# A hybrid SSD and mixture-of-experts block: TensorE's order in the expert part written out by the program

## The chip, the cores and the metric

The kernel runs on one core of a Trainium2 chip. The metric is the device time of one execution in microseconds (us). A profile of one execution gives the busy time, the waits and the order of the instructions on five engines: PE (TensorE, with its weight loads shown as PEld), DVE (VectorE), ACT (ScalarE), POOL (GpSimd) and SP (SyncE, which here only starts transfers).

## What is computed

One decoder block on 512 tokens of width 1024: adaLN and a mixer (Mamba-2 SSD beside a gated short convolution), then adaLN and a mixture of experts. The change lies in the second part, of which the core is:

```python
def moe_ffn(h, router_w, router_bias, w_gate, w_up, w_down, sh_gate, sh_up, sh_down):
    ...
    _, e_idx = lax.top_k(jnp.where(expert_mask, biased, -jnp.inf), TOP_K)
    ...
    def expert_block(args):
        xb, e = args
        return (jax.nn.silu(xb @ w_gate[e]) * (xb @ w_up[e])) @ w_down[e]

    yb = lax.map(expert_block, (xin, block_expert)).reshape(n_rows, d)
    routed = jax.ops.segment_sum(yb * row_gate[:, None], row_tok, num_segments=T + 1)[:T]
    shared = (jax.nn.silu(hf @ sh_gate) * (hf @ sh_up)) @ sh_down
```

There are 64 experts of inner width 256, each token goes to 8 of them, and all is float32.

## The kernel before

The first 870 us hold the mixer, the routing and the shared expert. The rest is the expert part. The experts are ranked by their number of tokens and each gets a capacity by its rank (`CAPS`). Blocks of 128 token rows are formed from them: one expert with 128 rows, or two to four experts that share a block. A *unit* (`units`, made in the order of the string `ORDER`) is one to three such blocks with their experts; there are 32 units and 41 blocks. The letters are kinds of units: a (96 and 32 rows), p (2 x 64), q (4 x 32), f (one whole block), and y, z, x (one or two whole blocks and a shared one).

A unit's weights come in *pieces* of 512 KB per expert (`piece`, L842 and L845): four for gate and up (two of the eight chunks of the contraction each), two for down. SP loads them into a ring of 14 pages in a fixed order: pieces 1 to 3 of a unit, piece 0 of the next, then the unit's down pieces. A page comes free when its last reader is through.

For a whole block, ScalarE and VectorE split each weight page into a high and a low part (`split`, L130 and L132), and `matmul3` makes three whole-array matmuls of them (L125 to L127). For a shared block, `tiled` (L883 to L888) gives each expert a strip of 64 or 32 columns of the array, and the strips can run at the same time; the matmuls of these strips are at L887. Then, per block, `act_t` (L865) makes silu(gate) x up on ScalarE (L868) and VectorE (L869) and transposes it on TensorE through a PSUM bank of the pair `tr` (L122); ScalarE copies it out (L878, or L130 where it is split). The down product follows, and `done` scales it and splits it into a ring of three results.

`combine` (L1098 to L1114) adds results to the output with whole-array matmuls against one-hot token matrices (L1106, L1107), into the two PSUM banks `y`, which VectorE adds to `res` (L1112). It ran as soon as two results were there (`GRP`). `need_x` (L1266) and `xsplit` (L848) transpose the gathered tokens of a block, and `slots` (L1031) finds the tokens of a later block and starts its gather on POOL (L1055). `beyond` counts what exceeds the capacities, for a loop that does not run here.

`ffn` (L890) is a generator with a yield after each of the four gate/up pieces. The list `steps` takes the generators in turn: pieces 1, 2 and 3 of a unit, piece 0 of the next, the unit's down product. But this list is not TensorE's order: a scheduler takes the instructions of all engines and places each engine's by priority and by its own estimate of times. So transposes, combines and matmuls of different units are interleaved at fine grain.

Of the kernel before, what the change touches and what calls it, by code (L numbers as in the profile page):

```python
# [31 lines left out]
GRP = 2  # L32
XA = 3
# [4 lines left out]
AHEAD = 14  # L38
# [3 lines left out]
BEY = 100  # L42
# [11 lines left out]
PSPLIT = (3,)  # L54
NPS = 0
# [8 lines left out]
def block_kernel(ctx: ExitStack, tc: tile.TileContext, a, out, dbg=None):  # L64
# [657 lines left out]
    for j in range(KD):  # L722
# [7 lines left out]
        sg = wk()  # L730
# [134 lines left out]
    def act_t(o, whole):  # L865

        sg = rt.tile([P, FE], F32, name="sg", bufs=2)
        S.activation(sg, o[:, :FE], AF.Silu)  # L868
        V.tensor_tensor(sg, sg, o[:, FE:], op=OP.mult)  # L869
        tp = bank("tr", 2)  # L870
        av = sg.rearrange("p (f j) -> p j f", j=2)
        for j in range(2):
            transpose(tp[:, j * P:(j + 1) * P], av[:, j, :])
        aw = wkp.tile([P, 4, P], F32 if whole else FR, name="wkr", tag="wk")
        ah, al = aw[:, 0:2], aw[:, 2:4]
        tv = tp[:, :256].rearrange("p (j n) -> p j n", j=2)
        if whole:
            S.activation(ah, tv, AF.Copy)  # L878
        else:
            split_to(ah, al, tv)  # L880
        return ah, al
# [8 lines left out]
    def ffn(blocks, xs, w, done, gp=()):  # L890


        es = sorted({e for b in blocks for e in b})
        split_e = sorted({b[0] for b in blocks if len(b) == 1})
        os_ = [bank(*(("pj", 3) if i < 3 else ("y", 2))) for i in range(len(xs))]
        for q in range(4):
            us = {e: w(e, q) for e in es}
            hl_ = {e: split(us[e], GP if gp is True or q in gp else None) for e in split_e}
            for o, (xh, xl), b in zip(os_, xs, blocks):
# [6 lines left out]
            if q == 3:  # L906
                acts = [act_t(o, len(b) > 1) for o, b in zip(os_, blocks)]
            yield
        us = [{e: w(e, 4 + j) for e in es} for j in range(2)]
# [155 lines left out]
    def expert(blocks, sl_, xs, w, gp=()):  # L1065
# [3 lines left out]
        def done(b, n, o):  # L1069
# [18 lines left out]
            if n == 1:  # L1088
                parts.append(res_[b])
                if len(parts) == GRP and not tail[0]:  # L1090
                    combine()
# [3 lines left out]
    parts = []  # L1095
# [212 lines left out]
    need_x(1)  # L1308
    running, i1 = {}, 0
    for i, (u, j) in enumerate(steps):  # L1310
        if j == 0:
            i0 = ublk[id(u)]
            i1 = i0 + len(u[1])
            need_x(i1)
            running[id(u)] = expert([b for b, _ in u[1]], sl[i0:i1], xs[i0:i1],
                                    lambda e, q, n=unum[id(u)]: take((n, e, q), AHEAD),
                                    PSPLIT if unum[id(u)] < NPS else ())
        if i + XA < len(steps) and steps[i + XA][1] == 0 and len(xs) == i1:
            need_x(i1 + 1)
        if i == BEY:  # L1320
            ostart, oend, obase, nov = beyond()
        tail[0] = i == len(steps) - 1
        next(running[id(u)], None)
    combine(True)
# [101 lines left out]
```

## Time and profile before

| | before |
| --- | --- |
| median of 3 runs | 1614.7 us (1608.26 to 1615.08) |
| the profiled execution | 1601.06 us |
| its span, first to last instruction | 1599.3 us |
| PE busy in the span | 1525.1 us (95%) |
| DVE, ACT, POOL busy | 978.3, 643.3 and 312.5 us (61%, 40%, 20%) |
| bytes moved by DMA | 335.82 MB, mean 210 GB/s |

The share of an engine is taken over stages with different limits, so it has to be read stage by stage. Matmuls overlap in the array, so the sum of their durations is more than the time they cover; what counts is the distance of their starts.

### The profile page before, as it was taken

To read this page: it belongs to the slowest core of one execution; us is meant where nothing else is said; L and a number is where in the kernel's file an instruction comes from. 1 tells how busy PE (TensorE), PEld (TensorE's weight loads), DVE (VectorE), ACT (ScalarE), POOL (GpSimd) and SP (SyncE) were. 2 spreads that over 40 slices of the span, in tenths; PEclk is the share of its full clock that TensorE was granted. 3 is DMA by queue.
4 is the path that set the end of the run, shared out by engine and by line. 5 is a ranking of instruction groups with operands and counts; after the bars stand their busy time and mean duration, and the time that the engine had idled before them with its cause. 6 is when DMAs were issued, how large, how long until landed. Compare 5 with 4: busy or idle time off the path is not lost. (4 is left out here: it accounts for less than half of the span.)

```text
span 1599.3 us, 24806 instructions
## 1 busy us (share of the span) xinstructions
PE 1525.1 (95%) x8253; PEld 1009.2 (63%) x8253; DVE 978.3 (61%) x1760; ACT 643.3 (40%) x926; POOL 312.5 (20%) x314
## 2 busy tenths in 40 slices
PE   6999899999999999999988899999999999999996
PEld 4688787787787877888765445454454445446643
DVE  5557778667868656536786354564464456447646
ACT  3556575555634545434441323142233123223323
POOL 0011111011001456400035121221111212111211
PEclk9999999999999999999989999999999999999998
DMA  9763333534340677626363989787999799899991
GB/s 277 178 166 94 101 78 80 147 84 101 105 116 17 195 222 223 174 79 199 151 211 100 289 280 367 268 311 212 343 322 315 247 365 334 245 333 328 360 316 66
DMA packets 240599, 335.82 MB, mean 210 GB/s; under 512 B 18548, under 2 KB 141780, under 8 KB 240468
## 3 DMA queue, kind: packets, MB, share of 16 engines
q1 hardware_dynamic: 229380, 303.75, 59.3%
q0 software_dynamic: 11088, 30.45, 7.0%
q8 instruction: 67, 1.10, 0.3%
q14 instruction: 64, 0.52, 0.1%
HBM read 334.58 MB, written 4.28 MB: 212 GB/s over the span
## 5 line engine op out<-in xcount | busy, mean ns | idle before, releaser
L132 DVE TENSOR_TENSOR wl<-pg,wh 128x1024 fp32r<-128x1024 f32 (+1 forms) x201 | 245.5, 1226 | 164.2 <-ACT wh L130 163.8
L130 ACT ACTIVATE wh<-pg 128x1024 fp32r<-128x1024 f32 (+1 forms) x207 | 202.2, 987 | 232.5 <-PE ps_pj L126 101.9
L125 PE MATMUL ps_pj<-hm,wh 128*128 128x512 f32 x680 | 274.6, 405 | 2.1 <-ACT wh L130 2.1
L127 PE MATMUL ps_pj<-hm,wl 128*128 128x512 f32 x680 | 267.0, 393 | 5.5 <-DVE wl L132 5.5
L126 PE MATMUL ps_pj<-hm,wh 128*128 128x512 f32 x680 | 266.4, 392 | 0.0
L887 PE MATMUL ps_pj<-pg,xt 128*32 128x512 f32 (+1 forms) x1472 | 247.7, 600 | 0.0
L125 PEld LDWEIGHTS ps_pj<-hm,wh 128*128 128x128 f32 x680 | 128.1, 188 | 36.2 <-issue 5.5
L127 PEld LDWEIGHTS ps_pj<-hm,wl 128*128 128x128 f32 x680 | 128.0, 188 | 35.5 <-DVE wl L132 8.3
L126 PEld LDWEIGHTS ps_pj<-hm,wh 128*128 128x128 f32 x680 | 128.0, 188 | 28.8 <-issue 3.4
L887 PEld LDWEIGHTS ps_pj<-pg,xt 128*32 128x32 f32 (+1 forms) x1472 | 63.4, 115 | 110.8 <-issue 101.8
L1112 DVE TENSOR_TENSOR res<-res,ps_y 128x512 f32<-128x512 f32 x152 | 102.6, 686 | 42.1 <-PE ps_y L1107 40.4
L1083 DVE SCALAR_TENSOR_TENSOR wk<-ps_y,red,pg 128x512 f32<-128x512 f32 x82 | 61.1, 748 | 88.1 <-PE ps_y L887 57.1
L1055 POOL DMA_INDIRECT pg<-h_d,idx x41 | 49.8, 1215 | 326.7 <-DVE oh L1039 78.5
L887 PE MATMUL ps_y<-pg,wkr 128*32 128x512 f32 (+1 forms) x736 | 107.5, 596 | 2.0 <-DMA pg<-in_w_down_dram 2.0
L1079 POOL TENSOR_SCALAR oht<-iota_t,tok 128x512 fp32r<-128x512 f32 x41 | 67.1, 1642 | 129.1 <-PE ps_y L1107 128.9
L1107 PE MATMUL ps_y<-pg,oht 128*128 128x512 f32 x224 | 89.4, 402 | 0.0
L338 POOL TENSOR_TENSOR pg<-pg 128x1024 f32<-128x1024 f32 x28 | 73.9, 2653 | 53.9 <-ACT pg L336 53.8
L868 ACT ACTIVATE sg<-ps_pj 128x256 f32<-128x256 f32 x44 | 16.9, 384 | 163.9 <-PE ps_pj L887 112.2
L122 PEld LDWEIGHTS ps_tr<-ident,pg 128*128 128x128 f32 x392 | 56.7, 191 | 34.4 <-ACT wkr L878 10.8
L125 PE MATMUL ps_pj<-pg,wh 128*128 128x512 f32 x192 | 75.0, 391 | 2.8 <-ACT zs L403 2.8
L127 PE MATMUL ps_pj<-pg,wl 128*128 128x512 f32 x192 | 75.3, 392 | 0.0
L122 PE MATMUL ps_tr<-ident,pg 128*128 128x128 f32 x392 | 68.6, 290 | 6.8 <-DMA pg<-h_d,idx 1.8
(383 smaller groups left out, 2550.9 us busy)
## 6 DMA issues: line engine op xcount, KB each, us to landing
pg<-in_w_gate_dram SPq DMA_DIRECT2D x256, 256.0 KB
pg<-in_w_up_dram SPq DMA_DIRECT2D x256, 256.0 KB
pg<-in_w_down_dram SPq DMA_DIRECT2D x128, 512.0 KB
pg<-in_w_in_dram SPq DMA_DIRECT2D x88, 512.0 KB
pg<-in_w_ada_dram SPq DMA_DIRECT2D x48, 512.0 KB
bc<-acs_d POOLq DMA_DIRECT2D x32, 256.0 KB, 5.2
pg<-in_w_ssd_out_dram SPq DMA_DIRECT2D x16, 512.0 KB
pg<-in_w_sc_out_dram SPq DMA_DIRECT2D x8, 512.0 KB
```

The costliest lines, as they stand in the source:

```text
L122: return PE.transpose(o, i, ident[:n, :n])
L125: PE.matmul(o, lh, rh, start=start, stop=False)
L126: PE.matmul(o, lh, rl, start=False, stop=False)
L127: PE.matmul(o, ll, rh, start=False, stop=stop)
L130: S.activation(hi, src, AF.Copy)
L132: V.tensor_tensor(lo, src, rw(hi), op=OP.subtract)
L338: GP.tensor_tensor(part[i], part[i], w, op=OP.add)
L887: PE.matmul(o[w * i:w * i + w, :], x[:, w * i:w * i + w], m, start=start, stop=stop, tile_position=(0, w * i))
L1079: GP.tensor_scalar(res_[b][0], iota_t, tok, None, op0=OP.is_equal)
L1083: V.scalar_tensor_tensor(yg, o, red[:, 1:2], g2b[:, ns_], op0=OP.mult, op1=OP.mult)
L1107: PE.matmul(o, oh_, yl[:, ns_], start=False, stop=(i == len(parts) - 1))
L1112: V.tensor_tensor(ra[t][:, ns_], ra[t][:, ns_], o, op=OP.add)
```

## The change

`act_t` is cut in two: `act_in` makes silu(gate) x up, right behind the last gate/up piece, and `act_t` its transpose, a step later. In `ffn` the blocks of a unit are taken in reverse order for the second and fourth piece, so that the same kind of matmul stands on both sides of a piece's end. `combine` is no longer called where the second result is ready. And TensorE's instructions in the expert part keep the program's order (`manual_schedule`), while the other engines are still placed by the scheduler. Per unit the order is now: pieces 1 to 3 of gate/up; piece 0 of the next unit; one stretch of whole-array work (the activation's transposes, the tokens of the unit after next, slots, and a combine when two results are there or the ring of three would not hold the unit's); the down product.

```diff
--- before.py
+++ after.py
@@ -30,7 +30,7 @@
 
 CAPS = ((1, 320), (4, 192), (3, 160), (4, 128), (16, 96), (13, 64), (21, 32)) + tuple((len(u), 128 // len(u)) for u in STAT)
 GRP = 2
-XA = 3
+NRING = 3
 NXG = 3
 
 
@@ -39,7 +39,7 @@
 NDEF = 2
 FORD = "q0 r0 s0 q1 r1 s1 q2 r2 s2 q3 r3 s3"
 NADA = 3
-BEY = 100
+BEY = 25
 ENG3 = ("PP", "VV", "VV", "VV")
 NWK = 5
 AD = "VVVV"
@@ -51,8 +51,6 @@
 LF = 0
 YAD = 4
 NSC = sum(f[1] == "sc" for f in FILL)
-PSPLIT = (3,)
-NPS = 0
 SPB = ((0, 0, 0), (0, 1, 0), (0, 0, 1), (0, 1, 1), (0, 0, 2))
 NSL = 2
 C_Z, C_X, C_B, C_C, C_DT = 0, 2048, 4096, 5120, 6144
@@ -862,11 +860,15 @@
                 split_to(hi[:, sl_, :], lo[:, sl_, :], tv)
         return hi, lo
 
-    def act_t(o, whole):
+    def act_in(o):
 
         sg = rt.tile([P, FE], F32, name="sg", bufs=2)
         S.activation(sg, o[:, :FE], AF.Silu)
         V.tensor_tensor(sg, sg, o[:, FE:], op=OP.mult)
+        return sg
+
+    def act_t(sg, whole):
+
         tp = bank("tr", 2)
         av = sg.rearrange("p (f j) -> p j f", j=2)
         for j in range(2):
@@ -890,13 +892,14 @@
     def ffn(blocks, xs, w, done, gp=()):
 
 
+
         es = sorted({e for b in blocks for e in b})
         split_e = sorted({b[0] for b in blocks if len(b) == 1})
         os_ = [bank(*(("pj", 3) if i < 3 else ("y", 2))) for i in range(len(xs))]
         for q in range(4):
             us = {e: w(e, q) for e in es}
             hl_ = {e: split(us[e], GP if gp is True or q in gp else None) for e in split_e}
-            for o, (xh, xl), b in zip(os_, xs, blocks):
+            for o, (xh, xl), b in list(zip(os_, xs, blocks))[::-1 if q % 2 else 1]:
                 for k in (2 * q, 2 * q + 1):
                     if len(b) == 1:
                         wh, wl = hl_[b[0]]
@@ -904,8 +907,10 @@
                     else:
                         tiled(o, xh[:, k, :], [us[e][:, :, k % 2, :] for e in b], k == 0, k == KD - 1)
             if q == 3:
-                acts = [act_t(o, len(b) > 1) for o, b in zip(os_, blocks)]
+                sgs = [act_in(o) for o in os_]
             yield
+        acts = [act_t(sg, len(b) > 1) for sg, b in zip(sgs, blocks)]
+        yield
         us = [{e: w(e, 4 + j) for e in es} for j in range(2)]
         wdn = {e: [split(us[j][e], GP if gp is True or 4 + j in gp else None) for j in range(2)] for e in split_e}
         for i, ((ah, al), b) in enumerate(zip(acts, blocks)):
@@ -1087,8 +1092,6 @@
                 S.activation(rt.tile([P, 1], F32, name="warm"), rw(yh)[:, 0:1], AF.Sqrt, bias=epsc, scale=0.0)
             if n == 1:
                 parts.append(res_[b])
-                if len(parts) == GRP and not tail[0]:
-                    combine()
 
         return ffn(blocks, xs, w, done, gp)
 
@@ -1305,23 +1308,39 @@
         V.scalar_tensor_tensor(obase, ostart, 128.0, caprow, op0=OP.mult, op1=OP.subtract)
         return ostart, oend, obase, nov
 
-    need_x(1)
-    running, i1 = {}, 0
-    for i, (u, j) in enumerate(steps):
-        if j == 0:
-            i0 = ublk[id(u)]
-            i1 = i0 + len(u[1])
-            need_x(i1)
-            running[id(u)] = expert([b for b, _ in u[1]], sl[i0:i1], xs[i0:i1],
-                                    lambda e, q, n=unum[id(u)]: take((n, e, q), AHEAD),
-                                    PSPLIT if unum[id(u)] < NPS else ())
-        if i + XA < len(steps) and steps[i + XA][1] == 0 and len(xs) == i1:
-            need_x(i1 + 1)
-        if i == BEY:
-            ostart, oend, obase, nov = beyond()
-        tail[0] = i == len(steps) - 1
-        next(running[id(u)], None)
-    combine(True)
+    running = []
+
+    def begin(n):
+
+        u = units[n]
+        i0 = ublk[id(u)]
+        i1 = i0 + len(u[1])
+        need_x(i1)
+        running.append(expert([b for b, _ in u[1]], sl[i0:i1], xs[i0:i1], lambda e, q: take((n, e, q), AHEAD)))
+        next(running[n])
+
+
+
+
+    with tc.manual_schedule(engines={mybir.EngineType.PE}):
+        begin(0)
+        need_x(ublk[id(units[1])] + len(units[1][1]))
+        for n, u in enumerate(units):
+            last = n + 1 == len(units)
+            for _ in range(3):
+                next(running[n])
+            if not last:
+                begin(n + 1)
+            next(running[n])
+            if n + 2 < len(units):
+                need_x(ublk[id(units[n + 2])] + len(units[n + 2][1]))
+            if n == BEY:
+                ostart, oend, obase, nov = beyond()
+            if len(parts) >= GRP or len(parts) + len(u[1]) > NRING or last and parts:
+                combine()
+            tail[0] = last
+            next(running[n], None)
+        combine(True)
 
 
     ocur = rt.tile([P, 1], F32, name="ocur")
```

How this moves instructions shows at three places. The first is TensorE in a unit with one whole block and one shared by two experts (`ps_pj_9885` and `ps_pj_9886` are its accumulators; `pg` are weight pages, `oht` the one-hot matrices). Before:

```order
L127 MATMUL ps_pj_9885<-wh1_78,xt_9753 128x512
L887 MATMUL ps_pj_9886<-pg_9727,xt_9845 64x512
L1107 MATMUL ps_y_9959<-pg_7275,oht_9932 128x512
L1106 MATMUL ps_y_9971<-pg_7075,oht_9735 128x512
L1107 MATMUL ps_y_9971<-pg_7076,oht_9735 128x512
L1106 MATMUL ps_y_9971<-rww_5869,oht_9932 128x512
L1107 MATMUL ps_y_9971<-pg_7275,oht_9932 128x512
L887 MATMUL ps_pj_9886<-pg_9795,xt_9845 64x512
L887 MATMUL ps_pj_9886<-pg_9727,xt_9845 64x512
L1106 MATMUL ps_y_9977<-pg_7075,oht_9735 128x512
```

Such a unit in the change (line numbers of the changed file; accumulators `ps_pj_9866` and `ps_pj_9867`):

```order
L125 MATMUL ps_pj_9866<-wh0_76,xt_9644 128x512
L889 MATMUL ps_pj_9867<-pg_9614,xt_9686 64x512
L889 MATMUL ps_pj_9867<-pg_9625,xt_9686 64x512
L120 MATMUL ps_tr_9895<-ident_95,sg_9863 128x128 x2
L120 MATMUL ps_tr_9901<-ident_95,pg_6528 128x128 x4
L120 MATMUL ps_tr_9907<-ident_95,pg_6528 128x128 x4
L1052 MATMUL ps_st_9916<-pay_5887,oh_9913 32x6
```

Before, the tiled matmuls of the two experts (`pg_9727` and `pg_9795`) are parted by matmuls of a combine, one of them alone on its strip; now the two experts' matmuls stand side by side and the whole-array work follows in one piece. (Two of the four tiled matmuls of the piece are shown; the others repeat them.) Over the expert part the order has 133 unbroken stretches of tiled matmuls before and 60 in the change.

The second place is TensorE at the start of the expert part (`ps_pj<-pg,xt` is gate/up of the first unit, `ps_st` the slots, `ps_tr<-ident,pg` the transposes of gathered tokens). Before:

```order
L122 MATMUL ps_tr<-ident,pg 128x128 x8
L887 MATMUL ps_pj<-pg,xt 64x512 x3
L1047 MATMUL ps_st<-pay,oh 32x6
L887 MATMUL ps_pj<-pg,xt 64x512 x2
L1047 MATMUL ps_st<-pay,oh 128x6
L887 MATMUL ps_pj<-pg,xt 64x512 x6
```

In the change:

```order
L1052 MATMUL ps_st<-pay,oh 128x6
L889 MATMUL ps_pj<-pg,xt 64x512 x4
L120 MATMUL ps_tr<-ident,pg 128x128 x8
L1052 MATMUL ps_st<-pay,oh 32x6
L889 MATMUL ps_pj<-pg,xt 64x512 x12
L889 MATMUL ps_pj<-pg,xt 32x512 x8
```

All but the first piece of the first unit, 12 of its 16 gate/up matmuls, now stands behind the transposes of the second unit's tokens.

The third place is ScalarE around the activation of a unit ahead of one with a whole block (`sg` is silu, `wkr` the copy of the transposed activation, `xt` of the transposed tokens, `wh` the high part of a weight page). Before:

```order
L868 ACTIVATE sg_9837<-ps_pj_9707 128x256
L878 ACTIVATE wkr_9843<-ps_tr_9840 128x256
L860 ACTIVATE xt_9845<-ps_tr_9846 128x512
L860 ACTIVATE xt_9845<-ps_tr_9852 128x512
L130 ACTIVATE wh1_78<-pg_9727 128x1024
L130 ACTIVATE wh2_80<-pg_9798 128x1024
```

In the change:

```order
L866 ACTIVATE sg_9863<-ps_pj_9624 128x256
L128 ACTIVATE wh1_78<-pg_9796 128x1024
L128 ACTIVATE wh2_80<-pg_9824 128x1024
L880 ACTIVATE wkr_9898<-ps_tr_9895 128x256
L858 ACTIVATE xt_9900<-ps_tr_9901 128x512
L858 ACTIVATE xt_9900<-ps_tr_9907 128x512
```

Two weight splits of the next unit now stand ahead of the copies. There are 9 units with one or two splits at this place, 13 splits together.

## Rows read from the trace of the kernel before

**Rows 1.** Windows: length, each engine's busy us (instructions), clock, DMA share, GB/s.

```profile
872.00:1572.00 700.00, 684.29 (x4102) 345.71 (x4105) 370.15 (x625) 199.24 (x318) 129.76 (x122) 1.00 0.88 300
...
1280.00:1480.00 200.00, 196.00 (x1350) 101.04 (x1342) 114.19 (x196) 59.93 (x93) 34.36 (x34) 1.00 0.94 321
```

**Rows 2.** Windows, line 887 alone (tiled matmuls): PE, PEld, clock, DMA share, GB/s.

```profile
872.00:1572.00 700.00, 353.44 (x2204) 92.32 (x2208) 1.00 0.88 300
```

**Rows 3.** Groups by shape, 872 to 1572 us: count, busy us, mean ns, idle before.

```profile
L887 PE MATMUL ps_pj<-pg,xt 128*32 128x512 f32 x1152 | 156.7, 597 | 0.0
...
L1112 DVE TENSOR_TENSOR res<-res,ps_y 128x512 f32<-128x512 f32 x152 | 102.6, 686 | 42.1 <-PE ps_y L1107 40.4 <-issue 1.1
...
L887 PE MATMUL ps_pj<-pg,xt 128*64 128x512 f32 x320 | 91.3, 612 | 0.0
...
L130 ACT ACTIVATE wh<-pg 128x1024 fp32r<-128x1024 f32 x72 | 75.0, 1054 | 102.6 <-DMA pg<-in_w_up_dram 41.9 <-DMA pg<-in_w_down_dram 27.7 <-PE ps_pj L127 22.9
...
L887 PE MATMUL ps_y<-pg,wkr 128*32 128x512 f32 x572 | 70.5, 596 | 2.0 <-DMA pg<-in_w_down_dram 2.0
...
L1106 PE MATMUL ps_y<-rww,oht 128*128 128x512 f32 x104 | 43.9, 424 | 2.7 <-ACT rww L130 2.7
...
L887 PE MATMUL ps_y<-pg,wkr 128*64 128x512 f32 x160 | 36.5, 598 | 0.0
```

**Rows 4.** Timeline of PE, 1234 to 1245 us: start, us, instruction, count.

```profile
1234.00 0.39 PE L127 MATMUL ps_pj<-wh,xt 128*128 128x512 f32 x1
...
1234.32 1.07 PE L887 MATMUL ps_pj<-pg,xt 128*64 128x512 f32 x2
...
1235.32 0.50 PE L1107 MATMUL ps_y<-pg,oht 128*128 128x512 f32 x1
...
1235.66 0.39 PE L1106 MATMUL ps_y<-pg,oht 128*128 128x512 f32 x1
...
1235.89 0.39 PE L1107 MATMUL ps_y<-pg,oht 128*128 128x512 f32 x1
...
1236.68 1.08 PE L887 MATMUL ps_pj<-pg,xt 128*64 128x512 f32 x4
...
1244.33 1.94 PE L887 MATMUL ps_pj<-pg,xt 128*64 128x512 f32 x8
```

**Rows 5.** Timeline of all engines, 1275 to 1277 us.

```profile
1275.38 0.38 ACT L868 ACTIVATE sg<-ps_pj 128x256 f32<-128x256 f32 x1 [10.87 <-PE ps_pj L887]
...
1275.80 0.42 DVE L869 TENSOR_TENSOR sg<-sg,ps_pj 128x256 f32<-128x256 f32 x1 [5.06 <-ACT sg L868]
...
1276.28 0.50 PE L122 MATMUL ps_tr<-ident,sg 128*128 128x128 f32 x2
```

**Rows 6.** Timeline of PE, start of the expert part.

```profile
872.38 1.93 PE L887 MATMUL ps_pj<-pg,xt 128*64 128x512 f32 x6
...
877.96 2.79 PE L887 MATMUL ps_pj<-pg,xt 128*64 128x512 f32 x12
...
882.60 1.18 PE L122 MATMUL ps_tr<-ident,pg 128*128 128x128 f32 x8 [1.85 <-DMA pg<-h_d,idx]
```

**Rows 7.** Windows, behind that wait (columns as in rows 1).

```profile
884.00:887.00 3.00, 3.00 (x6) 0.47 (x4) 0.00 (x0) 0.43 (x1) 0.00 (x0) 0.50 0.84 305
```

**Rows 8.** Lines 1283 and 1297 (`beyond`): ns of one, start of first and last.

```profile
L1283 PE MATMUL ps_st<-pm,wk x2: 272/296/320, 1346.3 to 1346.5; 64*128 64x64 f32 x2
L1297 PE MATMUL ps_st<-stri,xTs x1: 200/200/200, 1350.4 to 1350.4; 64*128 64x64 bf16 x1
```

**Rows 9.** Timeline of PE, the last unit's activation.

```profile
1564.80 0.50 PE L122 MATMUL ps_tr<-ident,sg 128*128 128x128 f32 x2
1565.77 0.50 PE L125 MATMUL ps_y<-wh,wkr 128*128 128x512 f32 x1 [0.47 <-ACT wkr L130]
```

**Rows 10.** Waits of SP's DMA queue, 872 to 1572 us: us, times, longest.

```profile
SPq L842 <- PE ps_pj L887: 65.2, 32, 9.4
...
SPq L845 <- PE ps_y L887: 40.7, 18, 12.0
```

## Prediction, made before the run

> **What bounds the kernel now.** I began with the slices of the page, to see which resource fills the last 730 us, then cut the time into windows, then took groups of instructions by shape, and last the timeline at the places where the change moves something. The chain of waits was no help: it ends in the last output rows. The slices show TensorE nearly full throughout and DMA rising in the second half. The windows put TensorE at 684.3 of the 700 us from 872 to 1572, the expert part, with DMA at 0.88; from 1280 to 1480 DMA is at 0.94 [rows 1]. So TensorE sets the end, and the loads are close behind it.
>
> But this busy share hides waste. The tiled matmuls alone cover 353.4 us [rows 2]. The reader is to compare that with what they need. Each fp32 matmul leaves two records, and the strips of a tile group run together: three tiled stretches of 64 columns take 1.07 us with two records, 1.08 us with four and 1.94 us with eight [rows 4]. So two and four records cost the same (a pair had lost its partner), and a half group costs (1.94 - 1.08) / 2 = 0.43 us. There are (1152 + 572) / 4 = 431 half groups in four strips (432 by the order) and (320 + 160) / 2 = 240 in two [rows 3]. 672 x 0.43 = 289 us, so 64 us go elsewhere: lost partners, the tails and edges of stretches, waits.
>
> **The change, term by term.** *Lost partners.* Putting each tiled matmul of the order on its column strips and counting a stretch by its fullest strip, I get 370 group times of 0.86 us before and 336, the least possible, in the change: 34 x 0.86 = 29.2 us saved.
>
> *Edges.* Whole-array matmuls stand 0.23 us apart. Around a tiled stretch the entry takes 1234.32 - 1234.00 = 0.32 (0.09 more), the stretch 1235.32 - 1234.32 = 1.00 against 0.86 (0.14 more), and the second matmul behind it 0.34 (0.11 more) [rows 4]: 0.34 us a round trip. The order has 133 tiled stretches before and 60 after: 73 x 0.34 = 24.8 us saved. Both savings lie on TensorE's own path, with nothing beside them: 54.0 us together.
>
> *Start of the expert part, which now waits.* Before, 26 tiled matmul records (four rows from 872.38 to 877.96) ran ahead of the transposes that wait 1.85 us for a gather at 882.60 [rows 6]. That is 13 half groups; now only the first piece, 4 half groups, stands ahead. 9 x 0.43 = 3.9 us lost, at least 0 (if the gather came early) and at most the 5.6 us of all thirteen. The wait also costs clock: from 884 to 887 the granted clock is 0.50, that is 1.2 GHz [rows 7], so 1.5 us, but that is there before too and cancels. Against the change speaks the Trainium skill, TensorE: Matmul & The Clock Gate, section on HAM oscillation: waits between bursts of matmuls let the clock fall, and the next burst starts slow. By that rule each of the new waits below would also cost this 1.5 us, and the sum would turn negative; by the rows only the longest waits do.
>
> *The overflow count (`beyond`)*. It has three matmuls in a chain with VectorE, the first at 1346.3 and the last at 1350.4 [rows 8]. Before, other matmuls ran in the gaps. In the program's order TensorE waits: 4.1 us less some 0.9 of its own work, 3.2 us lost, between 0 and 4.1.
>
> *Heads of the whole-array stretches.* The stretch begins with the transposes of the activation. Their input is late by a ScalarE and a VectorE step: 1275.38 to 1276.28, 0.90 us from the accumulator's end to the transpose [rows 5]. The next unit's first piece lies over it: 4 half groups, 1.72 us. So this costs nothing as long as both engines are free. Then come the transposes of gathered tokens, through the same two PSUM banks (`tr`), so the third waits for ScalarE's copy of the first. The nearest row is at 1565.77: 0.47 us idle for the copy of an activation, 0.97 us after its transposes began [rows 9]. Before, other work mostly filled this. I take 0.4 us for each of 32 units, 13 us; the ends are 0 and 32 x 0.97 = 31 us.
>
> *Combine.* Of the 19 combines in the expert part 14 have two blocks and 4 have three: four or six whole-array matmuls per bank (0.92 us or more) against 0.69 us of VectorE to empty it [rows 3], hidden. One has one block, 0.46 us: 8 fills x 0.23 = 1.8 us lost, between 0 and 4. In return the combine now stands ahead of the down product and reads results that are a unit old, so its waits for ScalarE's splits (2.7 us, rounded to 3) go [rows 3]: 3 us saved, between 0 and 3.
>
> *What ScalarE does first.* In its new order, at 9 units weight splits stand between the activation's silu and the copy that the transposes wait for: 13 splits in all. Each waits for a weight page, in order, and the copies behind it wait too. The 72 splits now wait 41.9 + 27.7 = 69.6 us for loads, 0.97 us each [rows 3]. 13 x 0.97 = 12.6 us lost. The ends are 0 (pages long there) and all 69.6 us.
>
> *Loads.* The order of SP's loads stays, apart from one read of the overflow count. I add nothing more for them, as a late load is already in the term before. The bound: in 1280 to 1480 TensorE would gain 54 x 200 / 700 = 15 us, where DMA's idle share leaves 0.06 x 200 = 12 us [rows 1]. So up to 15 us could be refused there.
>
> Shared expert, instruction counts of VectorE (eight combine adds fewer) and the moved silu cost nothing that a row shows.
>
> **Sum:** 54.0 - 3.9 - 3.2 - 13 - 1.8 + 3 - 12.6 = 22.5 us saved. The profiled execution took 1601.1 us (span 1599.3), 13.6 below the median of 1614.7; it would become 1579, and the median **1592 us**.
>
> **Rivals.** *All covers hold.* If the heads, the one-block combine and the splits cost nothing, 54.0 - 3.9 - 3.2 + 3 = 50 us are saved: 1565 us. For it: in the whole 700 us TensorE shows hardly 16 us without work [rows 1], although the same ScalarE queue stood behind it. Against it: then other work could fill gaps, now nothing can.
>
> *The loads take over.* SP's longest waits for a free page are on the tiled matmuls, 65.2 and 40.7 us [rows 10]. Long whole-array stretches free no page, long tiled ones free many at once; if the idle share of DMA therefore stays 0.12, the loads still take 616 / 0.88 = 700 us, and nothing is saved: 1615 us. Against it: 84 idle us are more than the forecast asks for.
>
> *Slower: ScalarE's order stops TensorE.* One mechanism: a weight page is late, ScalarE holds the activation's copy behind its split, and TensorE stands at the head of a stretch with all other work behind it. Without my 12.6 us for it the sum is 35.1 us saved, so it decides from 35 us on, 2.7 us for each of the 13 splits. With all 69.6 us of today's waits on the path it is 34 us slower: 1649 us. For it: some of the splits are for the unit after, whose pages are loaded behind the down pages of this one. Against it: a stretch that waits lets the loads catch up.
>
> *The clock.* Were each of 32 heads to bring 1.5 us at 1.2 GHz, 48 us would go: 25 us slower, 1640 us. The page on the clock gate named above would have it so. Against it: mean granted clock 1.00 over the part [rows 1], with the 0.47 us wait of [rows 9] in it.
>
> That the change does not do what it says is hardly possible, as the order shows 60 stretches for 133; it could be without effect only if the edges were not paid, 2 in 100.
>
> **How the numbers follow.** Forecast (10 to 35 us saved) 0.47; covers hold 0.18; loads 0.16; ScalarE's order 0.14; clock 0.03; no effect 0.02. The likeliest gives 1592 us. The range is 1567 to 1622 us: below it lies the extreme of the first rival, above it most of the slower two, under 2 in 10 together. About 0.5% (8 us) is what can be told from no change. Faster by more: the forecast, the first rival and 0.03 of the loads, 0.68. Within: 0.12 of the loads, no effect, and a little of ScalarE's order, 0.15. Slower: the rest, 0.17.
>
> **What would show it.** In the profile after, tiled matmuls should cover about 300 us instead of 353.4, and a timeline should show no tiled stretch of two records. The edges remain 0.34 us. The expert part should end some 20 us earlier, with DMA share at 0.90 or more. New idle time of TensorE should stand at transposes, put down to ScalarE's copies, of 13 us by the heads and 13 by the splits, and at the start at the gather, some 6 us. If the tiled matmuls still cover over 330 us, the first two terms are wrong; if idle time at the heads is beyond 50 us, the slower rival is right; if tiled matmuls wait for loads by more than 20 us, the loads are.

## The result, and the profile after

| | before | the change |
| --- | --- | --- |
| median | 1611.5 us of 4 runs (1607.96 to 1615.08) | 1656.3 us of 4 runs (1646.58 to 1658.43) |
| ratio | | 1.0266, 95% interval 1.0214 to 1.0318 |
| the profiled execution | 1601.06 us | 1658.43 us |
| its span | 1599.3 us | 1656.7 us |
| mean granted clock of the span | 0.988 | 0.965 |

The change is slower by 2.7%; 1592 us was forecast. To compare the two traces I cut the expert part from the last whole-array matmul of the shared expert to the last tiled one: 869.7 to 1572.6 us before, 881.3 to 1630.7 us after. Here are the windows of the change over that part and over the stretch of [rows 1]; columns as there.

```profile
881.30:1630.70 749.40, 673.83 (x4135) 352.15 (x4134) 371.51 (x620) 203.32 (x320) 123.98 (x124) 0.96 0.83 280
1280.00:1480.00 200.00, 189.12 (x1340) 98.33 (x1337) 104.82 (x174) 55.06 (x88) 36.85 (x37) 0.99 0.92 311
```

TensorE is busy for less time than before (673.8 us; 686.5 in the 702.9 us before), in a part that is 46.5 us longer. DMA's share fell from 0.88 to 0.83: the loads have room and yet, as will be seen, come too late. Line 889 alone, the tiled matmuls, answers to [rows 2]:

```profile
881.30:1630.70 749.40, 318.13 (x2208) 87.34 (x2208) 0.96 0.83 280
```

318.1 us for 353.4: that gain is there. What ate it are waits and the clock. The waits of TensorE from 870 to 1640 us (us in total, times, longest):

```profile
PE ps_tr L120 <- ACT wkr L880: 13.3, 10, 5.5
PE ps_tr L120 <- DMA pg<-h_d,idx: 11.1, 2, 8.4
PE ps_y L1109 <- DVE res L1115: 10.1, 10, 3.1
PE ps_tr L1296 <- DVE rb L1294: 8.1, 1, 8.1
PE ps_pj L123 <- ACT wh L128: 7.2, 5, 1.8
PE ps_pj L124 <- DVE wl L130: 3.8, 5, 0.8
PE ps_tr L120 <- DVE wkr L130: 3.4, 6, 1.1
PE ps_tr L120 <- DVE xt L130: 3.0, 6, 0.7
```

The longest of such waits before was 2.2 us. And the clock: the record of the granted clock has ten stretches at 0.50 (1.2 GHz) in this part, where before had two. Three of the ten, as windows with all engines:

```profile
927.00:933.80 6.80, 6.16 (x32) 2.24 (x36) 3.28 (x6) 3.05 (x6) 0.99 (x1) 0.50 0.96 277
954.30:964.50 10.20, 4.65 (x19) 4.04 (x20) 1.50 (x4) 1.19 (x2) 1.14 (x2) 0.50 0.59 214
1244.40:1247.80 3.40, 3.40 (x9) 2.64 (x8) 0.92 (x2) 0.00 (x0) 0.00 (x0) 0.50 0.30 120
```

Ahead of these three TensorE had waited 5.5, 8.4 and 2.6 us. The ten are 64.9 us long, TensorE is busy for 49.7 us of them, and half of that, 24.9 us, I count as lost (an estimate: from 1244 to 1247 us the combine's matmuls start 0.43 us apart, at full clock 0.23). Every run below is taken apart in this way: the part's length, its idle time (length less PE's busy time), the loss to the clock (half of the busy time at 0.50), and the rest, which I call work.

| run | median us | part | idle | clock | work |
| --- | --- | --- | --- | --- | --- |
| before | 1611 | 702.9 | 16.4 | 3.4 | 683.1 |
| the change | 1656 | 749.4 | 75.6 | 24.9 | 649.0 |
| e1, scheduler's order | 1599 | 694.1 | 23.1 | 7.7 | 663.3 |
| e2, own order, three engines | 1722 | 817.4 | 112.7 | 58.3 | 646.5 |
| e3, chains taken out | 1639 | 737.6 | 65.3 | 22.6 | 649.8 |
| e4, heads mixed with combines | 1661 | 751.3 | 70.6 | 32.3 | 648.4 |
| e5, own order mended | 1649 | 740.4 | 67.1 | 21.1 | 652.2 |
| e6, the same, TensorE alone | 1634 | 727.9 | 65.1 | 15.9 | 646.9 |
| e7, e1 and earlier gather | 1599 | 693.6 | 24.4 | 7.4 | 661.8 |
| e8, before and the combine's rule | 1598 | 691.4 | 21.3 | 3.4 | 666.7 |
| e9, the change, half the loads | 1616 | 709.4 | 52.0 | 17.3 | 640.0 |
| e10, before, half the loads | 1593 | 687.7 | 9.7 | 1.7 | 676.3 |
| e11, e5, half the loads | 1614 | 709.0 | 50.0 | 17.2 | 641.8 |
| e12, e5's program, scheduler's order | 1599 | 691.2 | 23.3 | 9.6 | 658.3 |

Each row is one profiled execution, and the runs of before lie up to 19 us apart (1599.35 to 1618.2 beside e5), so rows that differ by a few us are not told apart. The change did 34.1 us less work, and paid 59.2 us more in waits and 21.5 us more in clock: 46.6 us longer. The first 870 us, which the change does not touch, took 869.7 us in the profiled run of before and 873 to 884 us in all the others; these 11.6 us of the difference between the two profiled runs are not the change's.

**How a wait comes about.** The clearest place is a combine. These are rows of the timelines of ScalarE, VectorE and TensorE from 1236 to 1247 us:

```profile
1241.12 1.06 ACT L128 ACTIVATE wh<-pg 128x1024 fp32r<-128x1024 f32 x1 [6.32 <-DMA pg<-in_w_up_dram]
...
1242.21 1.22 DVE L130 TENSOR_TENSOR wl<-pg,wh 128x1024 fp32r<-128x1024 f32 x1 [2.75 <-ACT wh L128]
1243.35 1.28 DVE L1115 TENSOR_TENSOR res<-res,ps_y 128x512 f32<-128x512 f32 x2
...
1244.09 0.56 PE L1109 MATMUL ps_y<-pg,oht 128*128 128x512 f32 x1 [2.56 <-DVE res L1115]
1244.44 0.63 PE L1110 MATMUL ps_y<-pg,oht 128*128 128x512 f32 x1
```

A weight page is late; ScalarE has waited 6.32 us for it. VectorE's half of the split stands ahead of the combine's add, so the add, which needs no page, comes late too. The `y` bank is not emptied, TensorE waits 2.56 us for it, and its next matmuls take 0.63 us instead of the 0.39 us of [rows 4], as the clock is at half. At 922 us the same happens through ScalarE: two splits that wait for pages stand ahead of the copy `wkr`, and TensorE's transposes wait 5.5 us.

```profile
922.51 1.06 ACT L128 ACTIVATE wh<-pg 128x1024 fp32r<-128x1024 f32 x1 [4.21 <-DMA pg<-in_w_up_dram]
926.26 1.06 ACT L128 ACTIVATE wh<-pg 128x1024 fp32r<-128x1024 f32 x1 [2.69 <-DMA pg<-in_w_up_dram]
927.22 0.37 ACT L880 ACTIVATE wkr<-ps_tr 128x256 f32<-128x256 f32 x1
```

Even the overflow count was caught by it: three of its comparisons, of 0.22 us each, stood between VectorE's halves of three splits (1497 to 1504 us), for the first of which VectorE waited 3.3 us, and this turned a chain of 4.1 us [rows 8] into a wait of 8.1 us.

### The profile page after: what moved, and what is told of

The parts are those of the page before. It is cut to its first block, busy times and chain, and to the rows that moved or that the text cites. A ratio compares the mean times of both kernels' runs of the same rounds, so it can differ in the third digit from the quotient of the medians.

```text
span 1656.7 us, 24788 instructions
## 1 busy us (share of the span) xinstructions
PE 1518.5 (92%) x8253; PEld 1015.6 (61%) x8253; DVE 977.8 (59%) x1752; ACT 646.3 (39%) x926; POOL 305.1 (18%) x314
## 4 chain that ended last, share of the span: by engine, by line
PE 70%; DMA 12%; DVE 9%; ACT 4%; issue 2%; SPq 1%; POOL 1%; ACTq 0%; DVEq 0%; POOLq 0%
PE ps_pj L123 12%; PE ps_pj L125 12%; PE ps_pj L124 12%; PE ps_pj L889 8%; DMA pg<-in_w_up_dram 7%; PE ps_y L889 5%; PE ps_y L1109 4%; PE ps_y L1110 4%; PE ps_tr L120 3%; DVE wl L130 2%; DMA pg<-in_w_ada_dram 2%; PE ps_y L123 1%; ACT wh L128 1%; PE ps_y L125 1%; PE ps_y L453 1%
## 5 line engine op out<-in xcount | busy, mean ns | idle before, releaser
L123 PE MATMUL ps_pj<-hm,wh 128*128 128x512 f32 x680 | 277.8, 409 | 3.3 <-ACT wh L128 3.2
L124 PE MATMUL ps_pj<-hm,wh 128*128 128x512 f32 x680 | 268.6, 395 | 0.0
L889 PE MATMUL ps_pj<-pg,xt 128*32 128x512 f32 (+1 forms) x1472 | 215.0, 602 | 4.3 <-DVE sg L867 2.8
L123 PEld LDWEIGHTS ps_pj<-hm,wh 128*128 128x128 f32 x680 | 129.8, 191 | 38.3 <-ACT wh L128 6.2
L124 PEld LDWEIGHTS ps_pj<-hm,wh 128*128 128x128 f32 x680 | 129.6, 191 | 29.2 <-issue 3.4
L889 PEld LDWEIGHTS ps_pj<-pg,xt 128*32 128x32 f32 (+1 forms) x1472 | 59.4, 117 | 138.4 <-issue 123.9
L1115 DVE TENSOR_TENSOR res<-res,ps_y 128x512 f32<-128x512 f32 x144 | 97.9, 687 | 51.5 <-PE ps_y L1110 46.8
L1060 POOL DMA_INDIRECT pg<-h_d,idx x41 | 44.0, 1074 | 431.8 <-DVE idx L1057 160.4
L120 PE MATMUL ps_tr<-ident,pg 128*128 128x128 f32 x392 | 69.9, 307 | 36.3 <-ACT wkr L880 13.3
L128 ACT ACTIVATE hm<-wk 128x512 fp32r<-128x512 f32 (+1 forms) x66 | 28.6, 468 | 125.9 <-DVE wk L1088 99.1
L123 PE MATMUL ps_pj<-pg,wh 128*128 128x512 f32 x192 | 75.1, 391 | 2.0 <-ACT zs L401 2.0
```

The source lines that it names most:

```text
L120: return PE.transpose(o, i, ident[:n, :n])
L123: PE.matmul(o, lh, rh, start=start, stop=False)
L124: PE.matmul(o, lh, rl, start=False, stop=False)
L128: S.activation(hi, src, AF.Copy)
L889: PE.matmul(o[w * i:w * i + w, :], x[:, w * i:w * i + w], m, start=start, stop=stop, tile_position=(0, w * i))
L1115: V.tensor_tensor(ra[t][:, ns_], ra[t][:, ns_], o, op=OP.add)
```

## The experiments

The theories were: *no cover* (TensorE in a fixed order has nothing else to do while any of its inputs is late, and every wait counts); *queues* (the scheduler's order of ScalarE and VectorE, with splits ahead of short copies, makes the waits); *loads* (pages come too late); *chains* (the gather and the count are too long where they stand); and that the *other edits* cost.

**e1: TensorE's order given back to the scheduler, all else kept.**

```diff
-    with tc.manual_schedule(engines={mybir.EngineType.PE}):
+    if True:
```

> TensorE's order given back to the scheduler, every other edit of the change kept (activation in two steps, blocks in reverse order, the new rule for the combine, the count at unit 25). The order has 87 tiled stretches, against 133 before and 60 in the change. Theory 'order without cover' (the time is lost because TensorE may no longer do other work while it waits): idle time in the expert part falls from 76 to about 20 us, the clock is nearly full, and the fewer stretches save (133 - 87) x 0.34 = 16 us of work, so 1590 to 1600 us. Rival 'the other edits cost' (reverse order, combine rule, split activation): it stays at 1630 us or more.

1599.4 us, ratio to before 0.9942 (0.9924 to 0.9959). The other edits do not cost; they gain 19.8 us of work, against which stand 6.7 us more idle time and 4.3 of clock. What makes the change slow is one line, the fixed order. TensorE's waits now (the three longest groups):

```profile
PE ps_tr L120 <- DMA pg<-h_d,idx: 5.2, 2, 3.4
PE ps_tr L120 <- ACT wkr L880: 4.3, 2, 3.9
PE ps_pj L123 <- ACT wh L128: 3.3, 2, 1.7
```

**e2: the program's order on ScalarE and VectorE as well.** Its core (the pieces' splits are written apart from their matmuls, at most one piece ahead):

```diff
-    with tc.manual_schedule(engines={mybir.EngineType.PE}):
+    with tc.manual_schedule(engines={mybir.EngineType.PE, mybir.EngineType.Activation, mybir.EngineType.DVE}):
...
+            if 0 < q < 3:
+                prep(q + 1)
```

> TensorE's order as in the change, and ScalarE and VectorE keep the program's order too, with each weight split written at most one piece ahead of its matmuls and the down product's splits behind the activation's copies (no split stands between silu and the copy any more). Theory 'queues' (TensorE stands because the scheduler placed splits that wait for weight pages ahead of the short copies and adds that TensorE waits for): heads of the whole-array stretches from 25 to 10 us idle, the combine's waits for VectorE's adds from 10 to 4 us, half of the clock's loss of 25 us comes back: 1615 to 1630 us. Theory 'chains' (the waits are the gather's and the count's own length) or 'loads' (pages are simply late): less than 10 us gained, 1645 us or more.

1722.2 us, far outside. The waits that theory *queues* named did shrink: 3.2 us for `wkr` (13.3), 2.6 for the adds (10.1). Others took their place:

```profile
PE ps_st L1071 <- DVE oh L1063: 50.9, 20, 4.4
PE ps_pj L123 <- ACT wh L128: 23.2, 14, 2.8
PE ps_pj L124 <- DVE wl L130: 10.6, 15, 0.8
```

The one-hot matrix of a slot search, which depends on nothing late, now stood behind VectorE's subtractions, and the splits were written too late. The expectation had looked only at the waits that were there. This run says more of my order than of the theory.

**e3: the change with three chains out of the way.** The core (the count is also cut into three units' stretches, and unit 0's pieces go ahead of unit 1's tokens):

```diff
-            need_s(i + NXG)
+            need_s(i + NXG + 1)
...
+        yield
         xT = bank("tr", 2, BF)
```

> The change, with three chains taken out of TensorE's way: the gather of a block is issued one block earlier, unit 0's first pieces stand ahead of the transposes of unit 1's tokens, and the overflow count's three matmuls stand in three units' stretches instead of one. Waits of 11.1 us (gather) and 8.7 us (count) should go. Theory 'clock follows long waits': the half-speed stretches at 886, 954 and 1500 us go with them, 7 to 10 us more: 1624 to 1632 us. If the slow clock has nothing to do with these waits: 20 us and no more, about 1636 us. If loads bound the kernel, the waits come back elsewhere: 1645 us or more.

1639.0 us, ratio 1.0191 (1.0167 to 1.0215). The waits for gathers and for the count went, 19.8 us of them, but idle time fell by 10.3 only: the waits for `wkr`, the adds, the splits, the tokens and the pages grew by 9.6 us together. The clock gained 2.3 us instead of 7 to 10. The time fell by 17.3 us, nearest to the 1636 us of a clock that has little to do with these waits. Chains are a part, and half of what is taken out of one place comes back in the next.

**e4: the transposes written in turn with a combine in every unit.**

```diff
+            its = [combine_g() if parts else iter(()), heads(n)]
+            while its:
+                its = [g for g in its if next(g, END) is not END]
```

> The change, with a combine in every unit (of all results that are there) and its eight fills written in turn with the transposes of the activation and of the tokens; 60 tiled stretches as in the change, ScalarE's and VectorE's order still the scheduler's. If the idle time at the heads is the plain length of copy and subtraction (0.4 to 1.1 us each): 25 us falls to 5, the combine's waits of 10 to 3, and the clock gains 8 us: about 1620 us. If it is copies behind splits that wait for pages ('queues'): these waits are too long to be covered by one fill, 25 falls to 15 at best, with twelve more combines VectorE has 66 us more to do, and the time stays within 15 us of the change, 1640 to 1660 us.

1660.9 us, just past the upper end of what *queues* gave. The waits for `wkr` fell from 13.3 to 5.5 us, but those for the activation's product (`sg`) rose from 1.9 to 11.4 and those for the adds from 10.1 to 20.9, as VectorE had 12 combines more to do (435 us busy for 372).

**e5: e2 mended, and e6: the same program with TensorE alone in fixed order.** The core of e5 against e2; e6 is e5 with the engines of the change:

```diff
+            g = combine_g() if len(parts) >= GRP or len(parts) + len(u[1]) > NRING or last and parts else iter(())
+            next(g, None)
             next(running[n])
+            next(g, None)
...
+            if len(sl) < len(allb):
+                ohs.append(allb[len(sl)][1]())
...
-            need_s(i + NXG)
+            need_s(i + NXG + 1)
```

> As e2 (program order on TensorE, ScalarE and VectorE), with what e2 itself got wrong mended: the one-hot of a slot search is written one block ahead on VectorE, the next unit's second weight split stands ahead of the down product, the combine comes right behind the activation's transposes, the gather one block earlier, the count in three units' stretches, unit 0's pieces ahead of unit 1's tokens. TensorE still has 60 tiled stretches. Theory 'queues' (what stands ahead of a short copy or add on ScalarE and VectorE decides how long TensorE waits, so a good order there makes the fixed order pay): idle time of the expert part 75 to 30 us, loss by the clock 25 to 10 us: 876 + 649 + 40 + 27 = 1592, between 1580 and 1605 us. Theory 'no cover' (any fixed order waits, whatever the other queues do): idle time stays at 55 us or more, 1630 us and up.

> The program of e5, but only TensorE keeps the program's order; ScalarE and VectorE are placed by the scheduler again (12 splits stand between silu and copy in 8 units). It is the control for e5. Theory 'queues': the gains of e3 and no more, 1630 to 1640 us, with waits for the activation's copies and the combine's adds as in e3 (15 and 12 us). Theory 'emission' (the better written order does it, whoever keeps it): like e5.

e5 took 1649.1 us (ratio 1.026, 1.0187 to 1.0333), e6 1634.3 us (1.0174, 1.0103 to 1.0245). e6 lies where *queues* had put it (1630 to 1640 us), but e5 does not: with no split between silu and copy idle time is 67.1 us, where 30 was expected, and the control with the scheduler's queues does better. So *queues* fell as far as these orders go; that no better order exists is not shown. e5's waits:

```profile
PE ps_pj L123 <- ACT wh L128: 14.5, 10, 2.5
PE ps_y L1138 <- DVE res L1144: 8.5, 7, 2.1
PE ps_pj L124 <- DVE wl L130: 7.5, 10, 0.8
PE ps_tr L120 <- DVE xt L130: 7.1, 8, 2.6
```

Why the splits are late there, although their page is in, the timelines of VectorE, ScalarE and TensorE behind a down product show (1499 to 1506 us):

```profile
1499.78 0.74 DVE L1113 SCALAR_TENSOR_TENSOR wk<-ps_y,red,pg 128x512 f32<-128x512 f32 x1
1501.22 0.69 DVE L130 TENSOR_TENSOR pg<-wk,pg 128x512 fp32r<-128x512 f32 x1 [0.70 <-issue]
1501.83 0.74 DVE L1113 SCALAR_TENSOR_TENSOR wk<-ps_y,red,pg 128x512 f32<-128x512 f32 x1
1503.27 0.69 DVE L130 TENSOR_TENSOR pg<-wk,pg 128x512 fp32r<-128x512 f32 x1 [0.69 <-ACT pg L128]
1504.21 1.23 DVE L130 TENSOR_TENSOR wl<-pg,wh 128x1024 fp32r<-128x1024 f32 x1 [0.25 <-ACT wh L128]
...
1502.61 0.63 ACT L128 ACTIVATE pg<-wk 128x512 fp32r<-128x512 f32 x1 [1.42 <-DVE wk L1113]
1503.14 1.04 ACT L128 ACTIVATE wh<-pg 128x1024 fp32r<-128x1024 f32 x1
...
1504.23 0.51 PE L123 MATMUL ps_pj<-wh,xt 128*128 128x512 f32 x1 [1.77 <-ACT wh L128]
1505.49 0.50 PE L124 MATMUL ps_pj<-wl,xt 128*128 128x512 f32 x1 [0.75 <-DVE wl L130]
```

A piece of one whole block is 6 whole-array matmuls of 0.23 us, 1.4 us of TensorE, and asks VectorE for a subtraction of 1.23 us; just there VectorE also has the results of the down product to scale and split (4 instructions, 2.9 us, with gaps). ScalarE splits these results too, waits for VectorE at each, and comes to the weight's split only behind them. Over the whole part VectorE is half idle; in such a stretch it is not, and TensorE, which has only the whole block's matmuls in its order, stands.

**e7: e1 with the gather one block earlier.** The first edit of e3 in the kernel of e1.

> e1 (scheduler's order on all engines) with the gather of a block issued one block earlier. e1 waits 5.2 us for gathers at two places. If that wait sits on the path: 3 to 8 us less than e1 with the clock behind it, 1591 to 1596 us. If another wait (tokens, pages) is next behind it: within 3 us of e1, 1597 to 1601 us.

1599.1 us (0.9938, 0.9911 to 0.9965), no different from e1: the gather's 5.2 us fell to 1.5, the waits for `wkr` and `wh` grew from 7.6 to 12.6.

**e8: the kernel before with the combine's new rule alone.**

```diff
-                if len(parts) == GRP and not tail[0]:
-                    combine()
...
+        if j == 4 and (len(parts) >= GRP or len(parts) + len(u[1]) > len(ring) or i == len(steps) - 1 and parts):
+            combine()
```

> The kernel before with one edit of the change: the combine is called ahead of a unit's down product by the new rule, not in the middle of it; the scheduler orders everything. The order has 112 tiled stretches for 133. By the price of an edge, (133 - 112) x 0.34 = 7 us of work less, and as much again for lost partners: 1595 to 1602 us, half or more of what e1 gains. If e1's gain comes from the split activation and the reverse order: within 3 us of the kernel before.

1598.1 us (0.9933, 0.9899 to 0.9966). This one edit brings 16.4 us less work of the 19.8 of e1: nearly all that the change's edits are worth to a free order. The medians, 1598.1 and 1599.4 us, are not told apart.

**e9 and e10: half the loads, in the change and before; e11: in e5.** The core, the same in all three:

```diff
+    def both(n, e, q):
+        if e % 2 == 0:
+            held[n, e, q] = take((n, e, q), AHEAD)
+        return held[n, e - e % 2, q]
```

> The change with about half of the weight loads left out: of the experts that share a unit, the second takes the first one's page (and the fourth the third's), so those experts compute with wrong weights; every matmul, split and copy stays. Theory 'loads' (the splits and copies are late because their pages are): idle time of the expert part from 75 to 35 us or less, the clock's loss from 25 to 8 us, about 1600 us. Theory 'no cover' (copies, splits and adds have their own length, and TensorE in a fixed order has nothing else to do): at most 15 us of idle time goes, 1635 us or more.

> The kernel before with the same half of the loads left out, the control for e9. It waits some 9 us for pages on TensorE's path and has 16 us of idle time in all: 1600 to 1610 us under either theory. If the loads had bound it (a DMA share of 0.88 in this part): 1585 us or less.

> e5 (program order on three engines, mended) with the same half of the loads left out. Theory 'no cover': the waits for splits in units with one whole block (14.5 + 7.5 + 3.2 us), for the combine's adds (8.5 us) and at the heads (12 us) stay, 45 us or more of idle time, 1625 us or more. Theory 'loads': 20 us of idle time and 1600 us or less.

e9 took 1615.5 us (1.0054, 1.0029 to 1.0079), e10 1592.9 us (0.9897, 0.985 to 0.9943, two runs alone), e11 1614.2 us (1.003, 1.0009 to 1.005). So the change gains 40.8 us, before 15.5 us (more than either theory gave it), e5 34.9 us. e9 and e11 fall between *loads* and *no cover*. With all loads the change stands 44.8 us above the kernel before that ran beside it, with half of them (DMA shares of 0.53 and 0.56) 22.7 us: about half of the distance goes with the loads. In the row of groups for ScalarE's splits the change shows the loads' part, 116.6 us of waiting for pages where [rows 3] had 69.6:

```profile
L128 ACT ACTIVATE wh<-pg 128x1024 fp32r<-128x1024 f32 x72 | 76.1, 1057 | 128.4 <-DMA pg<-in_w_up_dram 84.1 <-DMA pg<-in_w_down_dram 32.5 <-PE ps_pj L125 6.2
```

What remains in e9 is not free of loads. TensorE's order there is that of the change, but the scheduler placed ScalarE's anew, with 22 splits between silu and copy for 13, and the three longest waits for `wkr`, 11.0 of 18.0 us, stand behind splits that still wait for a page. The longest:

```profile
1394.71 1.06 ACT L128 ACTIVATE wh<-pg 128x1024 fp32r<-128x1024 f32 x1 [5.35 <-DMA pg<-in_w_up_dram]
1395.67 0.36 ACT L880 ACTIVATE wkr<-ps_tr 128x256 f32<-128x256 f32 x1
...
1396.09 0.95 PE L120 MATMUL ps_tr<-ident,pg 128*128 128x128 f32 x4 [4.58 <-ACT wkr L880]
```

The cleaner pair is e5 and e11, where TensorE, ScalarE and VectorE keep the same order, instruction by instruction. In e11 neither TensorE nor ScalarE waits for a weight page any more, and still 50.0 us of idle time and 17.2 us of clock remain. These are not the loads'; they are waits for splits, copies and adds:

```profile
PE ps_y L1138 <- DVE res L1144: 8.5, 7, 2.1
PE ps_tr L120 <- DVE xt L130: 7.6, 9, 2.6
PE ps_pj L123 <- ACT wh L128: 7.1, 5, 1.8
```

Half the loads also let the ring of 14 pages reach further ahead. Whether pages come late because DMA is slow or because they are asked for late, these runs do not part.

**e12: e5's program, all engines ordered by the scheduler.**

> The program as written for e5, with the order of all engines given to the scheduler (86 tiled stretches). Theory 'no cover': it stands with e1 and e7, 1590 to 1602 us, since the same work has other work to cover its waits. Theory 'emission' (how the program is written decides): like e5, 1640 us or more.

1599.1 us (0.9931, 0.9909 to 0.9953). Word for word the program of e5 and e6; only who orders it differs, against e6 for TensorE alone. Work is within 12 us of theirs, idle time 23.3 us instead of 67.1 and 65.1. ScalarE's splits wait 64.8 us for pages in e12 too, so late inputs are still there, and TensorE does other work beside them. This is the cleanest pair for *no cover*. e1, e7, e8 and e12 all lie 0.6% or 0.7% below the kernel before and over 3% below the change, and are not told apart among themselves.

## Why the prediction was wrong, step by step

*The account.* The forecast had 54.0 us less work, 31.5 us more waits (the terms of the sum less the 3 us that the combine was to save) and nothing for the clock: 22.5 us faster. Measured in the expert part were 34.1, 59.2 and 21.5 us: 46.6 us slower. The error of 69.1 us is thus 19.9 us of work, 27.7 us of waits and 21.5 us of clock.

*What held.* The edges and lost partners are real, taken together; no run parts the two. Tiled matmuls cover 318 us, at a mean clock of 0.96, against 353 before and the some 300 of the forecast. Of the whole saving of 54.0 us, 34.1 came as less work. The term was too large by 20 us. Net of waits and clock, tiled matmuls (each counted up to the start of the next instruction) went from 340.7 to 305.2 us; I had priced those of before by their order at 370 x 0.86 + 133 x 0.23 = 349 us, more than they took. And the transposes went up, from 55.3 to 63.1 us, where I had seen no change.

*Heads and splits.* I had 13 + 12.6 = 25.6 us. The waits of the transposes and of the down product for `sg`, `wkr` and `xt` sum to some 25 us in the change, where before had about 3. Of these, 12.6 us stand behind a split that ScalarE ran between silu and copy, the very sum that was forecast, but at six of the nine units, one wait of 5.5 us among them: the mechanism was right, the exact agreement is luck.

*Combine: "hidden".* This step failed. I compared 0.92 us of matmuls with 0.69 us of VectorE's add per bank, as if the add always began at once. TensorE waited 10.1 us in ten places, and at each a weight's split stood ahead of the add on VectorE. At four of them, 7.5 us, VectorE had itself waited for ScalarE's half of the split; at the other six the split's own 1.2 us was enough.

*No term at all.* TensorE's waits for the split weights themselves (L123 and L124) were 11.0 us, where before had 3.7. The forecast saw splits only as something that stands ahead of copies.

*Start and overflow count.* 3.9 and 3.2 us were priced. The start held: TensorE waits 2.7 us for the gather there, 1.85 before, and 2.9 us for the slots, 1.1 before, some 3 us more together. The count's chain cost 8.7 us. And a second wait for a gather had no term: 8.4 us at 951 us, in a unit of three blocks, whose third gather is issued only when its first block has been transposed, all inside one stretch of TensorE's order. Before, the same chain lay beside tiled matmuls, and no row showed it.

*Loads: "I add nothing more for them".* This failed too. The order of the loads is the same and DMA has more idle time than before, but about half of the distance between the two kernels went with half of the loads. In a fixed order a page that comes late for one matmul holds all that follow. And the pages are asked for late: SP's waits for pages that tiled matmuls still hold, [rows 10], sum to 141.5 us before, to 180.9 us in the change and to 112.9 us in e1, the same program in the scheduler's order. The two longest groups in the change:

```profile
SPq L843 <- PE ps_y L889: 86.0, 28, 14.1
SPq L840 <- PE ps_y L889: 57.8, 7, 21.3
```

That TensorE, while it stands, frees no page, so that the next are asked for late as well, fits this; no run changed the ring to show it.

*The clock: "by the rows only the longest waits do".* This failed. I let the clock cancel, as if there would be no new long waits, while the sum itself contained 34.5 us of waits; and the rule, true of before, where the two half-speed stretches follow waits of 1.85 and 2.2 us, was too narrow. Two stretches at half speed became ten, and 3.4 us of loss 24.9. Three of the ten follow waits of 5.5, 8.4 and 8.1 us and cost 8.2 us; the other seven, 16.7 us, follow waits none of which is longer than 3 us. Over the runs the loss goes roughly with the idle time: 1.7 us at 10, 3.4 us at 16 and 21, 7 to 10 us at 23 or 24, 17 us at 50 and 52, 16 to 32 us from 65 to 76, 58 us at 113. The page of the Trainium skill that I had set against the change, TensorE: Matmul & The Clock Gate, section on HAM oscillation, names the cost: waits between bursts of matmuls bring slow bursts, on top of the wait. The trace agrees, with 24.9 us. But the section speaks of waits that are longer than the bursts between them; I had read it as a rule for every wait, the heads of 0.4 us too, which it does not state.

*The rivals.* The slower one (ScalarE's order stops TensorE, 1649 us, 0.14) and the clock (1640 us, 0.03) both came true in part and together; the loads (0.16) not as written, since DMA's share fell to 0.83, but as pages that come late. I had treated them as alternatives. As far as e1 and e12 show they have one cause, an order that cannot do anything else while it waits. The signs that I had set for them did not tell: some 25 us at the heads, under the 50, and 1.4 us of waits of tiled matmuls for loads, under the 20. Pages are waited for by ScalarE's splits, where none of these signs looks. The measured 1656 us lies above the range because its upper end was set by single mechanisms.

What I overlooked as a whole was in the profile: 16 us of idle time in 700, with VectorE's and ScalarE's queues full of waits (102.6 us before the splits alone, [rows 3]). I read that as proof that such waits are harmless. They were harmless because TensorE had other work beside them, as e12 against e6 shows.

## What to carry to other kernels

A low idle share of the bounding engine under a scheduler's order does not say that its inputs are on time; before an order is fixed, list the waits of the engines that feed it and ask which of them will have nothing beside it. Count a new wait twice, once as time and once as clock, and do not take only the long ones: most of the clock's loss here followed waits under 3 us. And look for gains in the order that leave the scheduler free: one moved call (e8) brought half of the work that the fixed order saved, and kept it.

## What was not expected of the hardware

Halving the loads of the kernel before gained 15.5 us, although TensorE's waits for pages and for weight splits in this part came to some 6 us. Its busy time fell by 8.4 us as well (686.5 to 678.1). e5 and e11 show the same with one order: the work falls from 652.2 to 641.8 us, and 9.7 us of that lie in the tiled gate/up matmuls (209.9 to 200.2 us), while the other groups stay within 1 us. So short delays of strips that go with the loads seem to lie inside what the trace counts as busy; whether the strips wait for their pages or run slower beside the transfers was not tried. And the clock fell behind short waits too: of the ten half-speed stretches of the change seven follow waits none of which is longer than 3 us, while the wait of 3.1 us for an add at 1577 us was followed by none. The length of a wait alone does not tell whether it costs clock; what else does was not tried.
